# Down projection of a two-layer encoder: plain blocks accumulate on the sum so far in PSUM, and the first mixer's index weights are split by one engine

## The chip, the cores and the metric

The kernel runs on one core of a Trainium2 chip, as one program. The metric is the device time of one execution in microseconds (us), the median of several runs; lower is better.

## What is computed

Two encoder layers over 512 tokens with a model width of 1024. Each layer is half a feed-forward network (FFN), a mixer, a cross-attention to a memory of 256 tokens, and a second FFN half. The change touches the end of all four FFNs and the start of the first mixer:

```python
def swiglu(x, wg, wu, wd):
    return (jax.nn.silu(x @ wg) * (x @ wu)) @ wd      # wd: 2816 x 1024

h = x
for layer in range(2):
    h = h + 0.5 * swiglu(rmsnorm(h, ffn1_norm), wg, wu, wd)
    h = h + mixer(rmsnorm(h, mix_norm), ...)           # layer 0: "even", layer 1: "odd"
    h = h + memory_xattn(rmsnorm(h, mem_norm), rmsnorm(mem, src_norm), ...)
    h = h + 0.5 * swiglu(rmsnorm(h, ffn2_norm), ...)
```

The even mixer starts with `h @ w_in`; the part of `w_in` for the index heads (`iq`, `ik`, `iw`) is the "index weights" below.

## The kernel before

The activations lie transposed: eight tiles `x[d]` of 128 features by 512 tokens, in float32. A float32 product is done as three matmuls on two-part numbers. Each operand is split into a high part (ScalarE rounds it: `wh`, `xh`, `hh`) and a low part (VectorE or GpSimd subtracts: `wl`, `xl`, `hl`), and TensorE sums high by high, high by low and low by high in a PSUM bank. There are eight banks, in two rings of four, `ps_pa` and `ps_pb`. TensorE's instructions keep the order in which the code is written; the other engines' instructions and the DMA issues are put in order when the kernel is built, by a scheduler that weighs readiness and priority. On the chip each engine then runs its own list in that order and waits at its head.

**The FFN.** The 2816 hidden features are 22 blocks, made two at a time: one pair plainly (`plain_pair`, L330), ten pairs with a seven-product scheme on quarters (`product`, L478). The down projection goes over the hidden blocks in three chunks of 8, 8 and 6. The first two chunks use the seven-product scheme and are summed by ScalarE and VectorE into eight SBUF tiles `f.sums[d]` (`gain`, L636 and L638). The third chunk is plain: for each of the eight outputs `d` (the "plain down blocks") `block` loads the 128x768 weights (L163) and splits them (L164, L166), `down_products` runs 18 matmuls into one bank (L718), and `done` finishes with three VectorE instructions:

- L738: `dn = bank + x`, where `x` is the sum of the first two chunks
- L739: `dn = dn * R`, the factor of the norm for each token
- L740: `x = 0.5 * dn + xr`, where `xr` is the residual, loaded back from DRAM

Block 0 is begun inside the last pair; its last two hidden blocks, and those of blocks 1 and 2, come once the pair's hidden values are ready. Then `made` starts the next norm: ScalarE makes `xh` (L212) and the square `sq` (L230), VectorE makes `xl` (L214), and GpSimd adds the squares up in `acc` (L231). SyncE parks each new `x` in DRAM (L186) and loads weights.

**What follows each FFN.** After the first, `mixer0`: five index weight tiles, each against all eight `x` (`index_gemm`, L1143), `x` 0 to 6 first for all three products, then `x` 7. After the second, the next FFN's `plain_pair` (L330): its first group takes the high weights of two tiles with `x` 0 to 3, then 4 to 6, then 7. After the third, `mixer1` (`gemm_nat`, L827), which takes the `x` two by two over many matmuls. After the fourth, the output is stored (L1606).

**Who splits the weights' low part.** `wload` gives it to VectorE, or, where `wshare` is n, every n-th tile to GpSimd (both L166). The table `WS` holds `wshare` for each part of the mixers; `WS[0]` is that of the index weights.

Of the kernel before, what the change touches and what calls it, by code (L numbers as in the profile page):

```python
# [11 lines left out]
F32 = mybir.dt.float32  # L12
# [3 lines left out]
OP = mybir.AluOpType  # L16
# [3 lines left out]
P = 128  # L20
S = 512
# [35 lines left out]
TOP_A = 3  # L57
TOP_B = 2
X_K = 2600
WS = (2, 3, 0, 1, 1, 2, 1, 2, 0, 0, 3, 2, 1, 1, 0, 3)  # L60
FIRST = (0, 1, -1, 2, 3, -2, 4, 5, 6, -3, -4, 7)

PAD_CONST = 24
# [10 lines left out]
HALF = 256  # L74
# [38 lines left out]
class Encoder:  # L113
# [583 lines left out]
    def block(self, c, d, own=False):  # L697

        nc, f = self.nc, self.f
        n = CHUNKS[c] * P  # L700
        src = self.I[f.pre + "wd"][d]
        if not own:
            return self.wload(src, n), self.bank2()
        with self.tc.high_priority():
            w = self.wp.tile([P, 1024], F32, name="wf", tag="wf", bufs=3)
            h, l = [f.tp.tile([P, WIDE], F32R, name=t, tag=t, bufs=1) for t in ("sh", "sl")]
            self.wfill((w, h, l), src, slice(0, n), nc.vector)
        return (h, l), self.bank2()

    def down_products(self, c, block, ops, tail):  # L710

        f = self.f
        (w, bank), nb = block, CHUNKS[c]
        for a, e in ops:
            for j in range(nb - 2, nb) if tail else range(nb - 2):
                b = sum(CHUNKS[:c]) + j
                h = f.H[b // 2][e][:, b % 2 * S:b % 2 * S + S]
                self.nc.tensor.matmul(bank, w[a][:, j * P:(j + 1) * P], h, start=j == a == e == 0,  # L718
                                      stop=j == nb - 1 and (a, e) == ops[-1])

    def reload(self):

# [8 lines left out]
    def down(self, c, first, olds):  # L731

        nc, f = self.nc, self.f

        def done(d, bank):
            x = self.x[d]
            t = f.tp.tile([P, 3 * HALF], F32, name="dn", tag="t")[:, :S]
            nc.vector.tensor_add(t, bank, x)  # L738
            nc.vector.tensor_mul(t, t, f.R)  # L739
            nc.vector.scalar_tensor_tensor(x, t, 0.5, olds[d], op0=OP.mult, op1=OP.add)  # L740
            self.made(d, x)

        early = [first, self.block(c, 1), self.block(c, 2)]
        for ops in (LEAD, REST):
            for b in early[1:]:
                self.down_products(c, b, ops, False)
        for d, b in enumerate(early):
            self.down_products(c, b, LEAD + REST, True)
            done(d, b[1])
        for d in range(len(early), KB):  # L750
            b = self.block(c, d)
            self.down_products(c, b, LEAD + REST, False)
            self.down_products(c, b, LEAD + REST, True)
            done(d, b[1])
# [530 lines left out]
    def xattn(self, pre, mp):  # L1285
# [77 lines left out]
        def gemm():  # L1363
            for h0 in (0, 2):
# [20 lines left out]
                if h0 == 0:  # L1385
                    self.wshare = WS[15]
            yield from self.out_proj(I[pre + "mem_wo"], 4, lambda k: parts[k] if k < len(parts) else None, (2,))
# [89 lines left out]
    def mixer0(self):  # L1477
        pre, I = "l0_", self.I
        with ExitStack() as ctx:
# [13 lines left out]
            def gemm():  # L1493
                iq = []
                self.wshare = WS[0]
                for j in range(4):
# [6 lines left out]
                b = []  # L1503
                yield from self.gemm_nat(b, w[0], xs, WS[1])
                bqk = self.heads(b, v, mp)
                b = []
                yield from self.gemm_nat(b, w[1], xs, WS[2])
                bv = self.values(b, r, P, mp)
                ready.append((bqk, bv))
                b = []  # L1510
                yield from self.gemm_nat(b, w[2], xs, WS[3])
                bqk = self.heads(b, v, mp)
                ready.append((bqk, bv))
                b = []
                yield from self.gemm_nat(b, w[3], xs, WS[4])
                aqk = self.heads(b, v, mp)
# [194 lines left out]
```

## Time and profile before

| what | us |
|---|---|
| median of 3 runs (2058.13 to 2061.13) | 2059.29 |
| the profiled execution | 2058.4 |
| its span, first to last instruction | 2056.6 |
| TensorE busy in the span | 2009.5 |
| VectorE busy | 1660.6 |
| ScalarE busy | 1224.0 |
| GpSimd busy | 395.0 |

TensorE is busy for 98% of the span, so the question of any change is which of its remaining waits it touches. The four plain down stages end at 338, 1060, 1389 and 2052 us of the span; the "first" to "fourth stage" below are these. In lists of instructions, a row is start, duration, engine, line, operation, output <- inputs, shape and count, and in brackets the engine's idle time ahead of it with what ended it.

### The profile page before, as it was taken

How to read it: one execution, taken by the hardware profiler on the slowest of the kernel's cores; microseconds unless marked ns; L12 is line 12 of the kernel's file. 1: busy time of each engine (PE TensorE's matmuls, PEld its weight loads, DVE VectorE, ACT ScalarE, POOL GpSimd, SP SyncE). 2: the span in 40 equal slices, each digit the busy share in tenths (PEclk: the TensorE clock that was granted, in tenths of full speed). 3: DMA queues.
4: the chain of work that ended last, by engine and by line, in shares of the span. 5: the costliest groups of instructions: out<-in, count | busy, mean ns of one | idle time of the engine just before them, and what ended most of it. 6: DMA issues, size and time to landing. Idle time of an engine off the chain costs nothing.

```text
span 2056.6 us, 35616 instructions
## 1 busy us (share of the span) xinstructions
PE 2009.5 (98%) x13982; PEld 1845.5 (90%) x13986; DVE 1660.6 (81%) x2533; ACT 1224.0 (60%) x1874; POOL 395.0 (19%) x352
## 2 busy tenths in 40 slices
PE   8999998999999999999999999999999999999998
PEld 7999997887778889999979999988888888999997
DVE  8979878479876889798799879786568777988976
ACT  6656554475586566565555656444778655666642
POOL 1012003435341211000020010014453122001000
PEclk9999999999999999999999999999999999999999
DMA  8777755322142267777557786835224324767672
GB/s 270 205 198 197 190 167 171 95 77 67 62 134 83 72 185 206 194 195 179 181 168 194 187 211 166 232 113 167 83 83 123 103 82 156 189 183 207 174 219 95
DMA packets 102184, 321.79 MB, mean 156 GB/s; under 512 B 11392, under 2 KB 14592, under 8 KB 102016
## 3 DMA queue, kind: packets, MB, share of 16 engines
q1 hardware_dynamic: 85888, 260.79, 38.3%
q0 software_dynamic: 16128, 58.73, 16.6%
q8 instruction: 110, 1.80, 0.3%
q14 instruction: 58, 0.48, 0.1%
HBM read 304.79 MB, written 14.68 MB: 155 GB/s over the span
## 4 chain that ended last, share of the span: by engine, by line
PE 87%; DVE 9%; ACT 2%; issue 1%; POOL 0%; DMA 0%; SPq 0%; DVEq 0%; ACTq 0%; POOLq 0%
PE ps_pa L478 35%; PE ps_pb L478 15%; PE ps_pa L827 11%; PE ps_pa L778 4%; PE ps_pa L330 3%; PE ps_pb L933 2%; PE ps_pa L718 2%; PE ps_pa L1377 2%; PE ps_pb L718 2%; PE ps_pb L985 1%; PE ps_pa L1224 1%; PE ps_pa L1143 1%; PE ps_pb L958 1%; PE ps_pb L778 1%; DVE xl L214 1%
## 5 line engine op out<-in xcount | busy, mean ns | idle before, releaser
L164 ACT ACTIVATE wh<-wf 128x1024 fp32r<-128x1024 f32 (+2 forms) x147 | 147.4, 1004 | 148.5 <-PE ps_pa L827 30.7
L454 ACT ACTIVATE wh<-s 128x1024 fp32r<-128x1024 f32 x140 | 149.1, 1065 | 124.7 <-PE ps_pa L478 55.9
L455 DVE TENSOR_TENSOR wl<-s,wh 128x1024 fp32r<-128x1024 f32 x140 | 171.3, 1223 | 39.2 <-ACT wh L454 36.7
L454 ACT ACTIVATE wh<-wf 128x1024 fp32r<-128x1024 f32 x124 | 131.9, 1064 | 104.3 <-PE ps_pa L478 52.1
L455 DVE TENSOR_TENSOR wl<-wf,wh 128x1024 fp32r<-128x1024 f32 x124 | 151.2, 1220 | 16.2 <-ACT wh L454 15.9
L166 DVE TENSOR_TENSOR wl<-wf,wh 128x1024 fp32r<-128x1024 f32 (+2 forms) x104 | 118.1, 1140 | 31.5 <-ACT wh L164 29.8
L166 POOL TENSOR_TENSOR wl<-wf,wh 128x1024 fp32r<-128x1024 f32 x43 | 104.4, 2428 | 149.0 <-ACT wh L164 138.2
L454 ACT ACTIVATE sh<-s 128x1024 fp32r<-128x1024 f32 x84 | 89.3, 1064 | 69.2 <-PE ps_pa L478 33.0
L455 DVE TENSOR_TENSOR sl<-s,sh 128x1024 fp32r<-128x1024 f32 x84 | 103.1, 1227 | 33.1 <-ACT sh L454 32.7
L827 PE MATMUL ps_pa<-wh,xh 128*128 128x512 f32 x384 | 123.7, 403 | 0.0
L827 PE MATMUL ps_pa<-wl,xh 128*128 128x512 f32 x384 | 119.8, 393 | 0.4 <-DVE wl L166 0.4
L827 PE MATMUL ps_pa<-wh,xl 128*128 128x512 f32 x384 | 119.9, 394 | 0.0
L478 PE MATMUL ps_pa<-xh,wl 128*128 128x256 f32 x672 | 103.8, 276 | 0.0
L478 PE MATMUL ps_pa<-xh,wh 128*128 128x256 f32 x672 | 103.7, 276 | 0.0
L478 PE MATMUL ps_pa<-xl,wh 128*128 128x256 f32 x672 | 103.6, 276 | 0.0
L231 POOL TENSOR_TENSOR acc<-acc,sq 128x512 f32<-128x512 f32 (+1 forms) x37 | 54.2, 1465 | 255.6 <-ACT sq L230 205.9
L499 POOL DMA_DIRECT2D s<-l_ffn_wq x40 | 35.1, 878 | 310.5 <-DMA s<-l_ffn_wq 172.6
L478 PEld LDWEIGHTS ps_pa<-xh,wh 128*128 128x128 f32 x672 | 89.1, 188 | 0.3
L478 PEld LDWEIGHTS ps_pa<-xh,wl 128*128 128x128 f32 x672 | 88.7, 188 | 0.2
L478 PEld LDWEIGHTS ps_pa<-xl,wh 128*128 128x128 f32 x672 | 88.7, 188 | 0.0
L827 PEld LDWEIGHTS ps_pa<-wl,xh 128*128 128x128 f32 x384 | 72.4, 189 | 17.3 <-DVE wl L166 1.5
L827 PEld LDWEIGHTS ps_pa<-wh,xl 128*128 128x128 f32 x384 | 72.8, 190 | 16.2
(417 smaller groups left out, 6009.0 us busy)
## 6 DMA issues: line engine op xcount, KB each, us to landing
wf<-l_ffn_wq SPq DMA_DIRECT2D x120, 512.0 KB, 4.7
s<-l_ffn_wq SPq DMA_DIRECT2D x80, 512.0 KB, 5.9
s<-l_ffn_wq POOLq DMA_DIRECT2D x80, 512.0 KB, 7.0
wf<-l_ffn_wdq SPq DMA_DIRECT2D x48, 512.0 KB, 3.6
wf<-l_w_in SPq DMA_DIRECT2D x48, 512.0 KB, 3.4
s<-l_ffn_wdq SPq DMA_DIRECT2D x32, 512.0 KB, 4.6
s<-l_ffn_wdq POOLq DMA_DIRECT2D x32, 512.0 KB, 6.9
parked<-x SPq DMA_DIRECT2D x48, 256.0 KB, 2.1
```

Source lines behind the costliest of these rows:

```text
L164: self.leading = nc.scalar.activation(wh[:, sl], w[:, sl], AF.Copy)
L166: eng.tensor_sub(wl[:, sl], w[:, sl], wh.bitcast(F32)[:, sl])
L231: self.summed = (eng or nc.gpsimd).tensor_add(acc[:, :n], acc[:, :n], sq[:, :n])
L330: nc.tensor.matmul(p, w[a][:, k * P:(k + 1) * P], xs[k][c], start=k == order[0] and a == c == 0, stop=k == order[-1] and a == 1)
L454: self.leading = nc.scalar.activation(h, t, AF.Copy)
L455: self.parted = nc.vector.tensor_sub(l, t, h.bitcast(F32))
L478: self.nc.tensor.matmul(bank[:, sl], w[a][:, o:o + P], xs[k][b], start=first and z == a == b == k == 0, stop=z == a == 1 and k == KB // 2 - 1,
L718: self.nc.tensor.matmul(bank, w[a][:, j * P:(j + 1) * P], h, start=j == a == e == 0, stop=j == nb - 1 and (a, e) == ops[-1])
L778: nc.tensor.matmul(banks[dd], a[:, o:o + P], parts(k)[b], start=k == first and a is wh and b == 0, stop=k == last and a is wl)
L827: nc.tensor.matmul(banks[i], xs[k][a][:, i * P:(i + 1) * P], w[b][:, kk * 512:kk * 512 + 512], start=k == a == b == 0, stop=k == KB - 1 an ...
L933: nc.tensor.matmul(bank[:, o:o + n], a, b[:, :n], start=c == 0, stop=c == len(ops) - 1)
L1377: nc.tensor.matmul(p, ws[z][a][:, k * P:(k + 1) * P], xs[k][b], start=k == order[0] and a == b == 0, stop=k == order[-1] and a == 1)
```

## The change

Each plain down block's PSUM bank is filled with `f.sums[d]` by a ScalarE copy ahead of its matmuls (`begun`, L714), and the matmuls add to it. So the addition of L738 goes. VectorE finishes with two instructions: L744 multiplies the bank by 0.5 and R, inside PSUM, and L745 adds the residual from PSUM into `x`. In the first mixer `WS[0]` goes from 2 to 0: VectorE makes the low part of all five index weight tiles.

```diff
-WS = (2, 3, 0, 1, 1, 2, 1, 2, 0, 0, 3, 2, 1, 1, 0, 3)
+WS = (0, 3, 0, 1, 1, 2, 1, 2, 0, 0, 3, 2, 1, 1, 0, 3)
...
         if not own:
-            return self.wload(src, n), self.bank2()
+            return self.wload(src, n), self.begun(d)
...
-        return (h, l), self.bank2()
+        return (h, l), self.begun(d)
+
+    def begun(self, d):
+
+        bank = self.bank2()
+        with self.tc.high_priority():
+            self.nc.scalar.copy(bank, self.f.sums[d])
+        return bank
...
-                self.nc.tensor.matmul(bank, w[a][:, j * P:(j + 1) * P], h, start=j == a == e == 0,
-                                      stop=j == nb - 1 and (a, e) == ops[-1])
+                self.nc.tensor.matmul(bank, w[a][:, j * P:(j + 1) * P], h, start=False,
+                                      stop=j == nb - 1 and (a, e) == ops[-1], skip_group_check=True)
...
         def done(d, bank):
             x = self.x[d]
-            t = f.tp.tile([P, 3 * HALF], F32, name="dn", tag="t")[:, :S]
-            nc.vector.tensor_add(t, bank, x)
-            nc.vector.tensor_mul(t, t, f.R)
-            nc.vector.scalar_tensor_tensor(x, t, 0.5, olds[d], op0=OP.mult, op1=OP.add)
+            nc.vector.scalar_tensor_tensor(bank, bank, 0.5, f.R, op0=OP.mult, op1=OP.mult)
+            nc.vector.tensor_add(x, bank, olds[d])
             self.made(d, x)
```

From the old line 715 on, the change's lines are numbered 5 to 7 higher. TensorE's order stays as it was; the lists of the other engines change near the four stages and in the first mixer's start.

VectorE at the end of the first stage, blocks 6 and 7, before:

```order
L738 TENSOR_TENSOR dn<-ps_pa,x 128x512
L739 TENSOR_TENSOR dn<-dn,R 128x512
L214 SCALAR_TENSOR_TENSOR xl<-x,cols,xh 128x512
L740 SCALAR_TENSOR_TENSOR x<-dn,xr 128x512
L166 TENSOR_TENSOR wl<-wf,wh 128x1024
L738 TENSOR_TENSOR dn<-ps_pb,x 128x512
L214 SCALAR_TENSOR_TENSOR xl<-x,cols,xh 128x512
L739 TENSOR_TENSOR dn<-dn,R 128x512
L740 SCALAR_TENSOR_TENSOR x<-dn,xr 128x512
L214 SCALAR_TENSOR_TENSOR xl<-x,cols,xh 128x512
L231 TENSOR_TENSOR acc<-acc,sq 128x512
```

And there, with the change:

```order
L744 SCALAR_TENSOR_TENSOR ps_pa<-ps_pa,R 128x512
L166 TENSOR_TENSOR wl<-wf,wh 128x1024
L745 TENSOR_TENSOR x<-ps_pa,xr 128x512
L214 SCALAR_TENSOR_TENSOR xl<-x,cols,xh 128x512
L744 SCALAR_TENSOR_TENSOR ps_pb<-ps_pb,R 128x512
L745 TENSOR_TENSOR x<-ps_pb,xr 128x512
L166 TENSOR_TENSOR wl<-wf,wh 128x1024
L214 SCALAR_TENSOR_TENSOR xl<-x,cols,xh 128x512
L231 TENSOR_TENSOR acc<-acc,sq 128x512
L166 TENSOR_TENSOR wl<-wf,wh 128x1024
```

Before, the low part `xl` of block 5 stood between the steps of block 6, and that of block 6 between those of block 7. Now each block's `xl` directly follows its `x`, apart from one index weight tile ahead of the last.

ScalarE in the first stage's last pair, with the change (L714 are the copies; `gs`, `hh` and `gu` belong to the pair's hidden values, `sh` and `wh` are weights):

```order
L557 COPY gu<-ps_pa 128x512
L714 COPY ps_pa<-x 128x512
L164 ACTIVATE sh<-wf 128x768
L561 ACTIVATE gu<-ps_pa 128x512
L164 ACTIVATE wh<-wf 128x768
L714 COPY ps_pb<-x 128x512
L597 ACTIVATE gs<-gs 128x512
L164 ACTIVATE wh<-wf 128x768
L578 ACTIVATE gu<-ps_pa 128x512
L376 ACTIVATE hh<-gs 128x512
L714 COPY ps_pa<-x 128x512
L597 ACTIVATE gs<-gs 128x512
```

The other rows stand there before too, in this order; the three copies are new, and five more stand in the list some 15 rows ahead of these.

ScalarE at the end of the second stage, blocks 5 to 7, before (the 128x1024 tiles are the next FFN's first two weights):

```order
L164 ACTIVATE wh<-wf 128x1024
L212 ACTIVATE xh<-x,cols 128x512
L230 ACTIVATE sq<-x 128x512
L164 ACTIVATE wh<-wf 128x1024
L212 ACTIVATE xh<-x,cols 128x512
L230 ACTIVATE sq<-x 128x512
L212 ACTIVATE xh<-x,cols 128x512
L230 ACTIVATE sq<-x 128x512
```

And there, with the change:

```order
L212 ACTIVATE xh<-x,cols 128x512
L230 ACTIVATE sq<-x 128x512
L164 ACTIVATE wh<-wf 128x1024
L212 ACTIVATE xh<-x,cols 128x512
L230 ACTIVATE sq<-x 128x512
L164 ACTIVATE wh<-wf 128x1024
L212 ACTIVATE xh<-x,cols 128x512
L230 ACTIVATE sq<-x 128x512
```

The first of the two weight tiles stood ahead of block 5's `xh` and now stands behind it; the second stood ahead of block 6's `xh` and now stands behind it.

## The prediction

> **What bounds the kernel now.** I read the page's head and its chain of waits first, then TensorE's waits, then the lists of instructions at the four stages.
>
> ```profile
> PE 2009.5 (98%) x13982; PEld 1845.5 (90%) x13986; DVE 1660.6 (81%) x2533; ACT 1224.0 (60%) x1874; POOL 395.0 (19%) x352
> PE 87%; DVE 9%; ACT 2%; issue 1%; POOL 0%; DMA 0%; SPq 0%; DVEq 0%; ACTq 0%; POOLq 0%
> ```
>
> TensorE is busy in 98% of the span and carries 87% of the chain. Its order and its matmuls stay. So the change can only give back what TensorE waits near the four stages, and the 5 us after its last matmul. Its waits, by what ended them (total, times, longest):
>
> ```profile
> PE ps_pa L330 <- ACT wh L164: 10.5, 4, 7.5
> PE ps_pa L1143 <- ACT xh L212: 5.9, 2, 3.3
> ```
>
> 7.5 of the first row's 10.5 us is one wait at the kernel's start; the second row is the end of the first stage. TensorE at the end of the first, where L1143 is the first index weight tile:
>
> ```profile
> 337.97 1.29 PE L1143 MATMUL ps_pa<-xh,wh 128*128 128x512 f32 x5
> 341.85 0.49 PE L1143 MATMUL ps_pa<-xh,wh 128*128 128x512 f32 x1 [2.58 <-ACT xh L212]
> 345.68 0.80 PE L1143 MATMUL ps_pa<-xh,wh 128*128 128x512 f32 x1 [3.34 <-ACT xh L212]
> 346.27 3.10 PE L1143 MATMUL ps_pa<-xl,wh 128*128 128x512 f32 x7
> 350.83 0.39 PE L1143 MATMUL ps_pa<-xh,wh 128*128 128x512 f32 x1
> ```
>
> Block 7's last matmul is issued just ahead of 337.97 and ends at 338.1. From 337.97 to 350.83 run the 21 matmuls on `x` 0 to 6. Unhindered they stand 0.227 us apart (below, eight take from 1076.24 to 1078.05), so 21 need 4.77 us: **8.1 us are lost**. 5.9 are the two waits in brackets, for `xh` of blocks 5 and 6. Most of the other 2.2 comes of a clock granted at half after them:
>
> ```profile
> 344.00:346.00 2.00, 0.32 (x1) 0.32 (x2) 2.00 (x4) 1.09 (x2) 0.00 (x0) 0.50 0.50 200
> ```
>
> (Columns: stretch, length, TensorE, its weight loads, VectorE, ScalarE, GpSimd, granted clock 0.50, DMA share, GB/s.) In the second stage, 48 matmuls of L330 lead to the group that starts at 1076.24:
>
> ```profile
> 1059.79 1.07 PE L330 MATMUL ps_pa<-xh,wh 128*128 128x512 f32 x4
> 1064.11 1.21 PE L330 MATMUL ps_pa<-xh,wh 128*128 128x512 f32 x4 [2.34 <-ACT wh L164]
> 1068.93 0.50 PE L330 MATMUL ps_pa<-xl,wh 128*128 128x512 f32 x1 [1.52 <-DVE xl L214]
> 1076.24 1.98 PE L330 MATMUL ps_pa<-xh,wh 128*128 128x512 f32 x8
> 1078.05 1.98 PE L330 MATMUL ps_pa<-xl,wh 128*128 128x512 f32 x8
> ```
>
> 48 steps of 0.227 are 10.9 us; it took 16.45: **5.55 us are lost**, 2.34 of it on a weight's high part on ScalarE, 1.52 on block 6's `xl`. The third stage loses one wait:
>
> ```profile
> 1390.45 0.73 PE L827 MATMUL ps_pa<-wl,xh 128*128 128x512 f32 x2 [0.42 <-DVE wl L166]
> ```
>
> Behind all three stands VectorE's queue. VectorE in the first stage, grouped (count, busy, mean ns, idle ahead), then some of its steps and a GpSimd row:
>
> ```profile
> L214 DVE SCALAR_TENSOR_TENSOR xl<-x,cols,xh 128x512 fp32r<-128x512 f32 x8 | 9.9, 1238 | 0.8 <-ACT xh L212 0.8
> L740 DVE SCALAR_TENSOR_TENSOR x<-dn,xr 128x512 f32<-128x512 f32 x8 | 8.6, 1078 | 0.1
> L739 DVE TENSOR_TENSOR dn<-dn,R 128x512 f32<-128x512 f32 x8 | 6.6, 822 | 0.1
> L738 DVE TENSOR_TENSOR dn<-ps_pa,x 128x512 f32<-128x512 f32 x4 | 2.8, 691 | 2.1 <-PE ps_pa L718 2.0
> ```
>
> ```profile
> 315.05 0.69 DVE L738 TENSOR_TENSOR dn<-ps_pa,x 128x512 f32<-128x512 f32 x1 [1.96 <-PE ps_pa L718]
> 338.30 2.74 DVE L740 SCALAR_TENSOR_TENSOR x<-dn,xr 128x512 f32<-128x512 f32 x1
> 344.80 1.21 DVE L166 TENSOR_TENSOR wl<-wf,wh 128x1024 fp32r<-128x1024 f32 x1
> 348.75 0.69 DVE L740 SCALAR_TENSOR_TENSOR x<-dn,xr 128x512 f32<-128x512 f32 x1
> ```
>
> ```profile
> 337.68 2.81 POOL L166 TENSOR_TENSOR wl<-wf,wh 128x1024 fp32r<-128x1024 f32 x1
> ```
>
> VectorE starts block 0 at 315.05 and ends block 7's `x` at 349.44, 34.4 us with 0.8 of idle, while TensorE is through with all eight at 338.1: the last `x` is 11.3 us late. L740 takes 1078 ns on average here. In the fourth stage, where GpSimd has nothing to do, it takes 692:
>
> ```profile
> L740 DVE SCALAR_TENSOR_TENSOR x<-dn,xr 128x512 f32<-128x512 f32 x8 | 5.5, 692 | 0.2
> L739 DVE TENSOR_TENSOR dn<-dn,R 128x512 f32<-128x512 f32 x8 | 5.5, 690 | 0.2
> ```
>
> The long ones stand beside GpSimd rows, as the 2.74 us at 338.30 beside the 2.81 at 337.68. L738, which reads PSUM and one SBUF tile, never is long: 691. So I count L744 and L745, each with one PSUM and one SBUF input, as never stretched.
>
> [...]
>
> **The change, part by part.**
>
> *Three instructions become two.* Starts follow each other at 0.60 us where they are independent and 0.73 where not (the fourth stage's last rows, below), 0.66 on average. Eight fewer: 5.3 us. L744 and L745 have no row: no VectorE instruction of the trace writes PSUM. L738 prices the reading at 0.69, and ScalarE shows what writing does to the same shape:
>
> ```profile
> L544 ACT COPY gu<-ps_pa x40: 554/567/581, 42.5 to 2007.8; 128x512 f32<-128x512 f32 x40
> L525 ACT COPY ps_pa<-ps_pa x36: 578/580/602, 50.7 to 1996.8; 128x512 f32<-128x512 f32 x36
> ```
>
> 580 against 567 ns. So I price both at 0.69, with 0.25 more for the pair as the upper bound, from the spread of L544 to L525 many times over. [...]
>
> *The stretches.* L740's is 8 x (1.078 - 0.692) = 3.1 us and L739's 8 x (0.822 - 0.690) = 1.1. Both are gone unless `xl` and `wl`, which keep two SBUF inputs, meet the GpSimd rows in their stead. Without that, VectorE needs 34.4 - 5.3 - 4.2 = 24.9 us and ends block 7 at 340.0; with all of it (or with L744 and L745 stretched after all), at 344.1. It cannot end before 338.14 + 0.73 + 0.69 = 339.6. I take 341.5, since some of the overlap will move: 3.4 us late in place of 11.3.
>
> *First stage.* Block 6 is then done by about 339, its `xh` is ready when TensorE wants it, near 339.5. `x` 7 is wanted at 338.0 + 4.77 = 342.8. Its `xh` comes 0.7 after `x`, and its `xl` stands behind an index weight's low part (1.21 at 344.80): 343.7. I take 0.6 us lost: **7.5 gained**; bounds 8.1 and, from 344.1, 4.8. Waits of this length leave the clock whole, as those of the second stage did (1.00 behind the wait of 2.34 us):
>
> ```profile
> 1064.00:1066.00 2.00, 1.90 (x8) 1.58 (x9) 2.00 (x2) 0.38 (x2) 1.08 (x1) 1.00 0.61 240
> ```
>
> *Second stage.* Here ScalarE's row decides:
>
> ```profile
> 1061.86 0.72 ACT L212 ACTIVATE xh<-x,cols 128x512 fp32r<-128x512 f32 x1 [3.37 <-DVE x L740]
> 1063.01 1.04 ACT L164 ACTIVATE wh<-wf 128x1024 fp32r<-128x1024 f32 x1
> ```
>
> The weight TensorE waits for stood behind block 5's `xh`. Now it stands behind block 6's `xh` and `sq`. `x` 6 comes some 2.5 us ahead of `x` 7 (two finishing steps, an `xl` and a 128x1024 low part lie between): by the first stage's bounds, from 1.0 before TensorE's end to 3.5 after it. From the start of `xh` to the end of the weight it is 2.2 us (1063.01 + 1.04 - 1061.86), and TensorE wants it after eight matmuls, at 1.8. The wait lies between none and 3.9 us; I take 1.2: **4.3 gained** (1.6 to 5.5).
>
> *Third and fourth.* The 0.4 us wait in the third goes (0 to **0.4**): that low part now stands ahead of block 6's last step. At the end one step goes:
>
> ```profile
> 2051.59 0.69 DVE L738 TENSOR_TENSOR dn<-ps_pb,x 128x512 f32<-128x512 f32 x1 [1.94 <-PE ps_pb L718]
> 2053.04 0.69 DVE L740 SCALAR_TENSOR_TENSOR x<-dn,xr 128x512 f32<-128x512 f32 x1
> ```
>
> The three start 0.73 apart: **0.7** (0.2 to 0.7, if the PSUM pair costs 0.25 to 0.5 more).
>
> *The copies.* Eight of 0.58 us per stage on ScalarE. TensorE needs each before its block, and each stands far ahead. They read sums that are finished with the second chunk, ahead of the last two pairs. Where ScalarE is dense:
>
> ```profile
> 298.77 0.84 ACT L164 ACTIVATE sh<-wf 128x768 fp32r<-128x768 f32 x1 [1.19 <-PE ps_pa L478]
> 307.49 0.63 ACT L597 ACTIVATE gs<-gs 128x512 f32<-128x512 f32 x1 [1.59 <-DVE gs L596]
> 310.22 0.63 ACT L597 ACTIVATE gs<-gs 128x512 f32<-128x512 f32 x1 [0.36 <-DVE gs L596]
> ```
>
> The copy ahead of `sh` fits into the 1.19 us of idle; that of block 7 into the 1.59 us ahead of the first `gs`; that of block 6 has 0.36 us ahead of the second `gs` and pushes it by about 0.2. What follows is the last `hl` on VectorE, and TensorE's use of it:
>
> ```profile
> 312.40 0.69 DVE L377 TENSOR_TENSOR hl<-gs,hh 128x512 fp32r<-128x512 f32 x1 [0.76 <-ACT hh L376]
> 374.11 0.69 DVE L260 TENSOR_REDUCE s<-ps_pb 128x4 f32<-128x512 f32 x1 [14.77 <-PE ps_pb L258]
> ```
>
> ```profile
> 313.95 0.61 PE L718 MATMUL ps_pa<-hl,sh 128*128 128x512 f32 x2
> ```
>
> It ends at 313.09, 0.86 before the use. So the copies cost **nothing**; gone is that cover if they lose over 0.9 us, and then TensorE waits directly, in each of four stages.
>
> *The index weights.* GpSimd's 2.81 us at 337.68 goes, which is part of the stretches above; VectorE takes over three of 1.21 us, in a time when it idles up to 14.77 us (the row at 374.11). Nothing.
>
> Sum: 7.5 + 4.3 + 0.4 + 0.7 = 12.9 us. The profiled execution took 2058.4: 2045.5. The median shown is 0.9 above it: **2046.4**. All the low bounds give 6.6, 2052.7; all the high ones 14.7, 2044.6.
>
> **The rivals.**
>
> *The overlap moves to `xl` and `wl`.* In the first stage every `xl` starts as its `sq` ends and GpSimd wakes, and L214 has the highest mean already, 1238. Then the low bounds hold: gains from 6.6 to 10, about 2051. Against it: a block then costs VectorE two steps, one `xl` and one 128x768 low part, some 2.9 us by starts, while TensorE needs 18 x 0.227 = 4.1; 1.2 us of slack absorbs a stretch. 24%.
>
> *No change.* If work inside PSUM were as slow as the 1.2 us of the 128x1024 rows, the pair would take 2.4 in place of 2.07, VectorE would gain 4.2 and lose 2.7, and 2 to 3 us would be left: 2056.5. The L738 rows speak against it. 8%.
>
> *Slower.* The copies hold ScalarE's queue in the last pair. Two copies stand between its halves, and one takes a bank that VectorE's last addition (L586) must leave first. Beyond the 0.86 us each microsecond is paid four times. To undo the 12.9 and add 4.1 it takes 4.3 + 0.9 = 5.2 us of delay per stage, nine copies' worth, 2063.5 and more. 4%.
>
> **How the numbers follow.** The forecast has 64%, the rivals 24, 8 and 4. A measurement here tells 0.2%, 4.1 us, from no change, so forecast and first rival are faster: 0.88; same 0.08; slower 0.04. The range takes in all the bounds and the runs' own spread of 1 to 2 us: 2043 to 2053.
>
> **What would show it.** The L1143 row after the stage should run without a bracket over 1 us and at clock 1.00, its group for `x` 7 starting about 5.4 us after block 7; the L330 wait for `wh` should be near 1 us; L744 and L745 should have minimum and maximum within 0.05 us of 0.69, also beside GpSimd rows; block 7's `x` should end some 3.4 us after TensorE; the row of `hl` ahead of L725's use should keep 0.5 us. It is wrong if L744 takes over 0.9, if L725 waits for a copy, or if the lost time turns up further on, as waits of L478 or L827 that were not there.

## The result: 15.9 us faster, and the profile after

| | before | after |
|---|---|---|
| median, four runs each | 2059.57 us (2058.13 to 2061.13) | 2043.68 us (2042.16 to 2044.55) |
| ratio, 95% interval | | 0.9922 (0.9905 to 0.9939) |
| profiled execution | 2058.4 | 2043.34 |
| its span | 2056.6 | 2041.6 |

A second series, five runs beside 21 of the kernel before, gave 2043.80 against 2059.64, a ratio of 0.9925 (0.9913 to 0.9938); 14 to 17 us were expected of it. The forecast was 2046.4, the range 2043 to 2053.

The page's head and its chain of waits, after: TensorE is busy 4.4 us less than the 2009.5 before (its mean granted clock is 0.998 in place of 0.996), VectorE 30 us less with 29 instructions fewer, ScalarE 16 us more.

```profile
PE 2005.1 (98%) x13982; PEld 1844.6 (90%) x13986; DVE 1630.7 (80%) x2504; ACT 1240.0 (61%) x1906; POOL 384.6 (19%) x349
PE 89%; DVE 7%; ACT 2%; issue 1%; DMA 1%; POOL 0%; SPq 0%; ACTq 0%; DVEq 0%; POOLq 0%
```

TensorE's waits, after. The row of the index weights on `xh` (5.9 us before) is gone. The row on `wh` has lost 2.4 us: 2.0 in the second stage, and 0.5 in the wait at the kernel's start (7.5 before), which the change does not touch. The row on `xl` was 3.0 us.

```profile
PE ps_pa L330 <- ACT wh L164: 8.1, 4, 7.0
PE ps_pa L330 <- DVE xl L214: 1.2, 4, 0.4
```

TensorE at the end of the first stage, L1148 now being the first index weight tile: 21 matmuls without a bracket, from 339.31 to 344.07, 4.76 us where it was 12.86. The window at this place grants the full clock (1.00, the third number from the right; it was 0.50).

```profile
339.31 1.75 PE L1148 MATMUL ps_pa<-xh,wh 128*128 128x512 f32 x7
...
344.07 0.40 PE L1148 MATMUL ps_pa<-xh,wh 128*128 128x512 f32 x1
```

```profile
344.00:346.00 2.00, 2.00 (x11) 1.61 (x10) 0.77 (x3) 1.21 (x2) 0.14 (x1) 1.00 0.85 266
```

The second stage, first group of L330: from 1051.94 to 1063.50 it takes 11.56 us, where it was 16.45. The wait for the weight's high part is down from 2.34 to 0.37.

```profile
1051.94 1.07 PE L330 MATMUL ps_pa<-xh,wh 128*128 128x512 f32 x4
1054.29 1.20 PE L330 MATMUL ps_pa<-xh,wh 128*128 128x512 f32 x4 [0.37 <-ACT wh L164]
1063.50 1.98 PE L330 MATMUL ps_pa<-xh,wh 128*128 128x512 f32 x8
```

VectorE in the first stage, grouped as before (count, busy, mean ns, idle ahead), then three of its rows. L744 and L745 are never long (675 to 700 ns in all four stages). The long ones now are some of `xl` (972 ns on average, 1308 before) and of the weights' low part (1151, 949 before). And `xl` waits for `xh`, 2.4 us in all, where it did not before: VectorE now has time to spare. `x` 7 ends at 342.25. The first two rows are those of before:

```profile
L214 DVE SCALAR_TENSOR_TENSOR xl<-x,cols,xh 128x512 fp32r<-128x512 f32 x7 | 9.2, 1308 | 0.0
L166 DVE TENSOR_TENSOR wl<-wf,wh 128x768 fp32r<-128x768 f32 x5 | 4.7, 949 | 0.0
```

```profile
L214 DVE SCALAR_TENSOR_TENSOR xl<-x,cols,xh 128x512 fp32r<-128x512 f32 x7 | 6.7, 972 | 2.4 <-ACT xh L212 2.4
L166 DVE TENSOR_TENSOR wl<-wf,wh 128x768 fp32r<-128x768 f32 x5 | 5.8, 1151 | 0.0
L744 DVE SCALAR_TENSOR_TENSOR ps_pa<-ps_pa,R 128x512 f32<-128x512 f32 x4 | 2.8, 693 | 2.0 <-PE ps_pa L725 2.0
L745 DVE TENSOR_TENSOR x<-ps_pb,xr 128x512 f32<-128x512 f32 x4 | 2.7, 683 | 0.0
```

```profile
321.96 1.79 DVE L214 SCALAR_TENSOR_TENSOR xl<-x,cols,xh 128x512 fp32r<-128x512 f32 x1
...
337.24 1.54 DVE L166 TENSOR_TENSOR wl<-wf,wh 128x1024 fp32r<-128x1024 f32 x1
...
341.56 0.69 DVE L745 TENSOR_TENSOR x<-ps_pb,xr 128x512 f32<-128x512 f32 x1
```

The fourth stage ends with two steps:

```profile
2037.24 0.70 DVE L744 SCALAR_TENSOR_TENSOR ps_pb<-ps_pb,R 128x512 f32<-128x512 f32 x1 [2.65 <-PE ps_pb L725]
2037.98 0.69 DVE L745 TENSOR_TENSOR x<-ps_pb,xr 128x512 f32<-128x512 f32 x1
```

Where the time went, between the profiled executions, by TensorE's starts: 8.1 us in the first stage, 4.9 in the second (16.45 - 11.56), 0.7 in the third (its first six matmuls take 1.36 us in place of 2.06, and the wait of L827 on `wl`, 0.42, has no row any more) and 0.7 at the end (from the first finishing step's start to the last one's 0.74 in place of 1.45). That makes 14.4 of the 15.0 us between the two spans. The other 0.6 is the balance of the rest: the change reaches its first index matmul 1.3 us later (339.31 against 337.97), and the parts between the stages give back 1.1, -0.2 and 1.1. Some of the 1.3 is two waits of L478 for `wh` and `wl`, 0.47 and 0.24 us at 174.85 and 176.28, which were not there before; they lie 110 us ahead of the first copy (285.27), and run 9 below, with twice the copies, has neither. Two profiled executions of the changed kernel differ by 1.0 (spans of 2041.6 and 2042.6), so none of the 0.6 is put down to the change.

### The profile page after: what moved, and what is told of

The parts are those of the page before. It is cut to its first block, busy times and chain, and to the rows that moved or that the text cites. A ratio compares the mean times of both kernels' runs of the same rounds, so it can differ in the third digit from the quotient of the medians.

```text
span 2041.6 us, 35601 instructions
## 1 busy us (share of the span) xinstructions
PE 2005.1 (98%) x13982; PEld 1844.6 (90%) x13986; DVE 1630.7 (80%) x2504; ACT 1240.0 (61%) x1906; POOL 384.6 (19%) x349
## 4 chain that ended last, share of the span: by engine, by line
PE 89%; DVE 7%; ACT 2%; issue 1%; DMA 1%; POOL 0%; SPq 0%; ACTq 0%; DVEq 0%; POOLq 0%
PE ps_pa L478 35%; PE ps_pb L478 15%; PE ps_pa L832 11%; PE ps_pa L783 5%; PE ps_pa L330 3%; PE ps_pa L725 3%; PE ps_pb L725 3%; PE ps_pb L938 2%; PE ps_pa L1382 2%; PE ps_pb L990 1%; PE ps_pa L1229 1%; PE ps_pb L963 1%; PE ps_pa L1148 1%; PE ps_pb L783 1%; PE ps_pb L330 1%
## 5 line engine op out<-in xcount | busy, mean ns | idle before, releaser
L166 DVE TENSOR_TENSOR wl<-wf,wh 128x1024 fp32r<-128x1024 f32 (+2 forms) x107 | 125.9, 1180 | 40.5 <-ACT wh L164 38.5
L166 POOL TENSOR_TENSOR wl<-wf,wh 128x1024 fp32r<-128x1024 f32 x40 | 97.2, 2429 | 153.2 <-ACT wh L164 142.4
L478 PE MATMUL ps_pa<-xh,wl 128*128 128x256 f32 x672 | 103.8, 276 | 0.0
L478 PE MATMUL ps_pa<-xh,wh 128*128 128x256 f32 x672 | 103.7, 276 | 0.0
L478 PE MATMUL ps_pa<-xl,wh 128*128 128x256 f32 x672 | 103.6, 276 | 0.0
L478 PEld LDWEIGHTS ps_pa<-xh,wh 128*128 128x128 f32 x672 | 89.1, 188 | 0.3
L478 PEld LDWEIGHTS ps_pa<-xh,wl 128*128 128x128 f32 x672 | 88.7, 188 | 0.1
L478 PEld LDWEIGHTS ps_pa<-xl,wh 128*128 128x128 f32 x672 | 88.7, 188 | 0.0
L832 PEld LDWEIGHTS ps_pa<-wl,xh 128*128 128x128 f32 x384 | 72.3, 188 | 15.9
```

What stands on the lines that cost most here:

```text
L166: eng.tensor_sub(wl[:, sl], w[:, sl], wh.bitcast(F32)[:, sl])
L478: self.nc.tensor.matmul(bank[:, sl], w[a][:, o:o + P], xs[k][b], start=first and z == a == b == k == 0, stop=z == a == 1 and k == KB // 2 - 1,
L832: nc.tensor.matmul(banks[i], xs[k][a][:, i * P:(i + 1) * P], w[b][:, kk * 512:kk * 512 + 512], start=k == a == b == 0, stop=k == KB - 1 an ...
```

## The experiments

Each was run five times or more beside the kernel before, on the same chip. The questions: which of the two savings on VectorE, fewer instructions or no stretches, brings the gain; what the index weights add; whether the stretches that moved to `xl` and `wl` still cost; and what covers the copies.

**1. The down blocks alone.** `WS[0]` stays at 2.

```diff
-WS = (0, 3, 0, 1, ...)
+WS = (2, 3, 0, 1, ...)
```

> The down blocks of the change alone; the first mixer's index weights keep GpSimd. Theory of the prediction (fewer VectorE instructions and no stretched finishing steps both count, the index weights add nothing by themselves): the GpSimd row of 2.81 us near 337.7 stays, but L744 and L745 beside it stay at 0.69, so it stretches at most an xl or a wl; 13.5 to 15.5 us below the kernel before, within 1.5 us of the whole change. Rival (the index weights carry a good part of the first stage's 8.1 us): 8 to 12 us below, with a wait for xh or xl of 1 us or more at the first index weight tile.

Measured: 2044.45 against 2058.95, 14.5 us faster, ratio 0.993 (0.9918 to 0.9943). TensorE in the first stage:

```profile
341.28 1.75 PE L1148 MATMUL ps_pa<-xh,wh 128*128 128x512 f32 x7
...
346.22 0.49 PE L1148 MATMUL ps_pa<-xh,wh 128*128 128x512 f32 x1
347.00 0.50 PE L1148 MATMUL ps_pa<-xl,wh 128*128 128x512 f32 x1 [0.29 <-DVE xl L214]
```

`x` 7 ends 1.2 us later than in the change, measured from the first L1148, and TensorE loses 0.2 us ahead of its group and 0.7 behind it (0.29 in the bracket). The down blocks are the change.

**2. The index weights alone.** The kernel before, with `WS[0] = 0`.

> The index weights of the first mixer by VectorE alone, the down blocks as before. Theory of the prediction: the 2.81 us GpSimd row goes and with it the stretch of L740 at 338.30 (2.74 to 0.69), but three more VectorE rows of 1.21 come into its queue, one of them ahead of the last x: between 1 us slower and 2 us faster than before, all of it in the first stage. Rival (the index weights carry a good part): 3 to 6 us faster, the 3.34 us wait for xh gone and the clock whole.

Measured: 2058.14 against 2058.95, ratio 0.9997 (0.9988 to 1.0006): no difference that can be told. TensorE and VectorE in the first stage:

```profile
342.96 0.50 PE L1143 MATMUL ps_pa<-xh,wh 128*128 128x512 f32 x1 [1.55 <-ACT xh L212]
346.74 0.80 PE L1143 MATMUL ps_pa<-xh,wh 128*128 128x512 f32 x1 [3.28 <-ACT xh L212]
```

```profile
344.18 1.75 DVE L740 SCALAR_TENSOR_TENSOR x<-dn,xr 128x512 f32<-128x512 f32 x1
```

The stretch of 2.74 us is gone: block 5's L740 takes 0.68 at 341.47. But an index weight's low part of 1.21 (340.34) now stands ahead of it. The next GpSimd addition stretched block 5's `xl` before (1.79 at 342.48) and now stretches block 6's L740 (1.75). The wait ahead of block 5's matmul fell by 1.0 us, the one ahead of block 6's stayed.

**3. As few instructions, but through SBUF.** The change with the product written to an SBUF tile, and with `WS[0]` at 2: it is run 1 with this one difference, not the whole change as the text below says. The first step then has PSUM as its input and SBUF as its output, the second reads two SBUF tiles.

```diff
-WS = (0, 3, 0, 1, ...)
+WS = (2, 3, 0, 1, ...)
...
-            nc.vector.scalar_tensor_tensor(bank, bank, 0.5, f.R, op0=OP.mult, op1=OP.mult)
-            nc.vector.tensor_add(x, bank, olds[d])
+            t = f.tp.tile([P, 3 * HALF], F32, name="dn", tag="t")[:, :S]
+            nc.vector.scalar_tensor_tensor(t, bank, 0.5, f.R, op0=OP.mult, op1=OP.mult)
+            nc.vector.tensor_add(x, t, olds[d])
```

> The whole change, but the first finishing step writes its product to an SBUF tile, so that the second reads two SBUF inputs, as the last step did before: as few instructions as the change, and still open to a stretch. Theory of the prediction: the instruction count saves 5.3 us of VectorE a stage, up to 3.1 of stretch come back in the second step; block 7's x ends 343 to 345 in the first stage, and the kernel is 8 to 13 us faster than before. Rival (all of it comes from the stretches): L745 at 1.0 us or more on average and 2 to 5 us faster.

Measured: 2045.04, 13.9 us faster, ratio 0.9932 (0.9919 to 0.9946); a little more than expected. The second step is stretched again in the first stage (869 ns, in run 1 679 to 684), and `x` 7 ends at 343.54, as expected; TensorE waits 0.54 us. Against run 1 that is 0.5 us more lateness of `x` 7 (4.66 for 4.13, table below), and a time that cannot be told from it (13.9 for 14.5).

```profile
L214 DVE SCALAR_TENSOR_TENSOR xl<-x,cols,xh 128x512 fp32r<-128x512 f32 x7 | 8.0, 1142 | 1.6 <-ACT xh L212 1.6
L746 DVE TENSOR_TENSOR x<-dn,xr 128x512 f32<-128x512 f32 x8 | 6.9, 869 | 0.1
```

```profile
344.34 0.49 PE L1149 MATMUL ps_pa<-xh,wh 128*128 128x512 f32 x1 [0.54 <-ACT xh L212]
```

**4. As many instructions, none with two SBUF inputs.** The kernel before, its three steps inside the bank; no copies, `WS[0]` at 2.

```diff
-            nc.vector.tensor_add(t, bank, x)
-            nc.vector.tensor_mul(t, t, f.R)
-            nc.vector.scalar_tensor_tensor(x, t, 0.5, olds[d], op0=OP.mult, op1=OP.add)
+            nc.vector.tensor_add(bank, bank, x)
+            nc.vector.tensor_mul(bank, bank, f.R)
+            nc.vector.scalar_tensor_tensor(x, bank, 0.5, olds[d], op0=OP.mult, op1=OP.add)
```

> The kernel before, but its three finishing steps work in the PSUM bank, so that none has two SBUF inputs: as many instructions as before, none open to a stretch; no copies, index weights by GpSimd as before. Theory of the prediction: 4.2 us of VectorE are saved a stage and block 7's x ends near 345 in the first stage; 5 to 9 us faster than before, and nothing of the 0.7 us at the end. Rival (all of it comes from the stretches): 12 to 15 us faster, both stalls gone. Rival (the count alone): 0 to 2 us.

Measured: 2047.28, 11.7 us faster, ratio 0.9945 (0.9932 to 0.9957): above the 5 to 9 of my theory, just below the rival's 12 to 15. TensorE's wait in the first stage, and the three steps, L737 to L739 here, without a stretch:

```profile
344.50 0.49 PE L1142 MATMUL ps_pa<-xh,wh 128*128 128x512 f32 x1 [1.15 <-ACT xh L212]
```

```profile
L738 DVE TENSOR_TENSOR ps_pb<-ps_pb,R 128x512 f32<-128x512 f32 x4 | 2.8, 690 | 0.0
L739 DVE SCALAR_TENSOR_TENSOR x<-ps_pb,xr 128x512 f32<-128x512 f32 x4 | 2.7, 677 | 0.0
```

By the time alone the first rival stays possible, since the interval is 8.9 to 14.0 us; but it asked for both stalls to be gone, and 1.15 us of waiting is left in the first stage and 0.93 (on `xl`) in the second, and run 3 came to 13.9 with stretches left. So neither rival holds: **each of the two edits by itself brings most of the gain**, and they do not add up. Why is seen below.

**5. No GpSimd additions.** The kernel before, and (run 6) the change, with GpSimd's additions of the squares behind the down blocks left out. Beside the first stage's finishing steps that leaves one GpSimd row in the kernel before, the index weight's (2.88 us at 335.71), and in the change, where all GpSimd rows there are such additions (321.33 to 342.10), none.

```diff
+            if eng is not None or not getattr(self, 'quiet', False):
-            self.summed = (eng or nc.gpsimd).tensor_add(acc[:, :n], acc[:, :n], sq[:, :n])
+                self.summed = (eng or nc.gpsimd).tensor_add(acc[:, :n], acc[:, :n], sq[:, :n])
...
+            self.quiet = True
             self.made(d, x)
+            self.quiet = False
```

> The kernel before without GpSimd's additions of the squares behind the down blocks; the norms after the four stages then lack the squares of all blocks but those that VectorE adds, and the output changes with them. VectorE keeps its three finishing instructions. Theory of the prediction (stretches and count both count): no L740, L739 or L214 over 1.0 us in the four stages but beside the index weight's GpSimd row, block 7's x ends 4 to 6 us after TensorE in the first stage, and the kernel is 9 to 13 us faster than before, without the 0.7 us at the end. Rival (the count is what matters): 5 us faster or less.

Measured, for the kernel before without the additions: 2045.67 against 2059.64, 14.0 us faster, ratio 0.9934 (0.992 to 0.9947), above the 9 to 13 expected. Its VectorE in the first stage (L740 and L741 are the second and third step here):

```profile
L740 DVE TENSOR_TENSOR dn<-dn,R 128x512 f32<-128x512 f32 x8 | 6.8, 847 | 0.1
L741 DVE SCALAR_TENSOR_TENSOR x<-dn,xr 128x512 f32<-128x512 f32 x8 | 5.5, 688 | 0.1
L214 DVE SCALAR_TENSOR_TENSOR xl<-x,cols,xh 128x512 fp32r<-128x512 f32 x7 | 5.2, 743 | 0.0
```

`xl` takes 743 ns in place of 1308 in the same stretch of the kernel before, the last step 688 in place of 1078. The second step's 847 holds the one row beside the index weight's GpSimd row, 1.98 us at 337.16. So the long rows come from GpSimd's additions and that index row, by taking them away.

**6. The change without the GpSimd additions.**

> The changed kernel without GpSimd's additions of the squares behind the down blocks, so that nothing of xl or of the weights' low parts can be stretched there; the norms after the four stages lack most of their squares, and the output changes with them. Theory of the prediction (the stretches that moved to xl and wl are absorbed, TensorE is what bounds): xl at 0.75 throughout, VectorE through with block 7 by 1 to 2 us earlier, and the time within 1 us of the change. Rival (the overlap moved and still costs): 2 to 5 us faster than the change.

Measured: 2043.55 against 2059.14, ratio 0.9924 (0.9911 to 0.9936), the change's own time. `xl` is down from 972 to 749 ns, `x` 7 ends 1.3 us earlier, and the first group of the second stage loses nothing any more (10.88 us for its 48 matmuls), yet that is worth only the 0.66 us that the change still lost there. The first rival, an overlap that moves and goes on costing, had the move right and the cost wrong.

```profile
L214 DVE SCALAR_TENSOR_TENSOR xl<-x,cols,xh 128x512 fp32r<-128x512 f32 x8 | 6.0, 749 | 2.5 <-ACT xh L212 2.4
```

**7. The copies alone.** The kernel before with the copies, the matmuls still starting each block by overwriting.

> The kernel before with the copies into the banks added; the matmuls still begin each block by overwriting, so the copies do nothing but take ScalarE's time. Theory of the prediction: the last hl still ends 0.3 us or more ahead of its use, and the time is within 1 us of the kernel before. Rival (the copies hold ScalarE's queue): 2 us or more slower, with a wait at L718 in each of the four stages.

Measured: 2059.77 against 2059.64, ratio 1.0001 (0.9992 to 1.001). No cost, to within the interval of some 2 us either way, and the last `hl` ends 0.85 us ahead of its use (313.50 against 314.35).

**8. Each copy four times.** The change, with three more copies per bank.

```diff
-            self.nc.scalar.copy(bank, self.f.sums[d])
+            for _ in range(4):
+                self.nc.scalar.copy(bank, self.f.sums[d])
```

> The changed kernel with each copy into a bank made four times over. In the trace of the change the last hl ends 0.86 us ahead of its use. Three more copies of about 0.53 by starts stand ahead of the second gs, 1.6 us. Theory of the prediction (beyond the cover each microsecond is paid in all four stages): hl comes 0.7 to 1.4 us late, a wait on it at L725's matmuls with hl in each stage, and the kernel is 3 to 6 us slower than the change. Rival (the copies have more room than that, or the planner sets them elsewhere): within 1 us of the change.

Measured: 2063.89 against 2059.64, ratio 1.0021 (1.0012 to 1.003): 20.1 us slower than the change, against 3 to 6 expected, so the rival fell as well. TensorE's waits, and its rows ahead of the first stage:

```profile
PE ps_pa L478 <- ACT gu L544: 8.8, 6, 1.9
PE ps_pa L726 <- ACT sh L164: 8.2, 4, 2.7
```

```profile
299.40 0.73 PE L478 MATMUL ps_pa<-t3h,sh 128*128 128x256 f32 x4 [1.87 <-ACT gu L544]
...
305.13 1.35 PE L726 MATMUL ps_pa<-hh,sh 128*128 128x512 f32 x4 [2.73 <-ACT sh L164]
306.28 1.91 PE L726 MATMUL ps_pa<-hl,sh 128*128 128x512 f32 x4
307.99 1.75 PE L726 MATMUL ps_pa<-hh,sl 128*128 128x512 f32 x4
309.58 0.63 PE L478 MATMUL ps_pb<-xh,wh 128*128 128x256 f32 x4
```

```profile
306.00:308.00 2.00, 2.00 (x7) 1.51 (x6) 1.09 (x3) 1.22 (x3) 0.00 (x0) 0.50 0.41 65
```

It isn't `hl` that comes late but, ten microseconds earlier, `gu` (8.8 us of waits in place of 1.3) and `sh` (8.2 in place of 1.9): the extra copies stand among the last pair's high parts, two of them right ahead of `sh`:

```profile
303.21 0.58 ACT L715 COPY ps_pb<-x 128x512 f32<-128x512 f32 x1
303.72 0.58 ACT L715 COPY ps_pa<-x 128x512 f32<-128x512 f32 x1
304.24 0.84 ACT L164 ACTIVATE sh<-wf 128x768 fp32r<-128x768 f32 x1
```

The wait of 2.73 us is then followed by half a clock (0.50 from 306 to 308): 12 matmuls take 4.45 us, in the change 2.86 (301.00 to 303.86). The first stage starts its index matmuls 6.0 us later than the change does (345.35 against 339.31): 1.87 + 2.73 - 0.48 (a wait that the change has too) + 1.59 is 5.71 of it.

**9. Each copy twice.** After run 8 I took the 0.19 us of idle ahead of `sh` to be the true cover, all but used up.

> The changed kernel with each copy into a bank made twice. Four copies each cost 20 us, and TensorE then waited for gu and for sh, not for hl. In the change's trace ScalarE has 0.19 us of idle left ahead of sh, which TensorE awaits already (0.48 us). Theory that the cover lies there and is as good as used up: one more copy pushes sh by 0.3 to 0.9 us in every stage, and the kernel is 1.5 to 6 us slower than the change. Theory of the prediction (the cover is the 0.86 us ahead of hl's use): one more copy fits, within 1 us of the change.

Measured: 2043.16 against 2059.14, ratio 0.9925 (0.9911 to 0.9938): as the change, so that theory fell too. ScalarE around `sh`:

```profile
298.50 0.59 ACT L715 COPY ps_pa<-x 128x512 f32<-128x512 f32 x1
299.24 0.84 ACT L164 ACTIVATE sh<-wf 128x768 fp32r<-128x768 f32 x1 [0.15 <-PE ps_pa L478]
300.00 0.58 ACT L715 COPY ps_pa<-x 128x512 f32<-128x512 f32 x1
```

The second copy simply stands behind `sh` (300.00), where ScalarE has time. So 16 copies a stage fit and 32 do not; where between the two the cover ends wasn't tried.

## Why the prediction was right, and where its numbers were off

The forecast's gain was 12.9 us, and all its upper bounds together 14.7 (2044.6). Measured are 15.9 by the medians and 15.1 between the profiled executions, of which the four places named give 14.4. So the range held only by the 1 to 2 us that it allowed for the spread, and what lies above the 14.4 is luck as far as these runs show. The mechanism held in all four places.

The table puts the runs side by side, each gain against the kernel before in its own series. "x 7 late" is the end of the last finishing step of block 7 less the start of the first index matmul; "lost" is TensorE's time from its first matmul to the group for `x` 7 less 4.77 us in the first stage, and over the 48 matmuls less 10.9 in the second.

| kernel | gain, us | x 7 late | lost, 1st | lost, 2nd |
|---|---|---|---|---|
| before | | 11.47 | 8.09 | 5.55 |
| index weights alone | 0.8 | 10.40 | 6.74 | 5.54 |
| three steps in PSUM | 11.7 | 5.26 | 1.30 | 1.53 |
| before, no GpSimd additions | 14.0 | 5.23 | 1.27 | 0.16 |
| two steps through SBUF | 13.9 | 4.66 | 0.69 | 0.71 |
| down blocks alone | 14.5 | 4.13 | 0.17 | 0.64 |
| the change | 15.8 | 2.94 | 0.00 | 0.66 |
| the change, no GpSimd additions | 15.6 | 1.62 | 0.00 | 0.00 |

- **What bounds, and the mechanism: right.** The first stage follows one line. The matmul on block 7's `xh` can start 0.80 us behind `x` 7 and is due 4.77 us after the first index matmul, so 3.97 us of lateness are free and the rest is lost: 5.26 gives 1.29 (1.30 measured), 5.23 gives 1.26 (1.27), 4.66 gives 0.69 (0.69), 4.13 gives 0.16 (0.17), 2.94 gives none. The 0.80 is read from these four kernels, so their agreement shows that block 7's `xh` is what that matmul starts on in each, no more (in run 5 TensorE had already lost 0.79 us of it to block 6's `xh`). For 11.47 the line gives 7.50 of 8.09, for 10.40 6.43 of 6.74; there the wait for block 6 and the half clock behind it (0.50 from 346 to 348 before, from 347 to 349 in run 2) end later. This is why the two savings do not add up: 7.5 us of lateness had to go, the fewer steps through SBUF took 6.8 of it (run 3), the bank in place of SBUF by itself 6.2 (run 4), both 7.3 (run 1), both with the index weights 8.5, and the last 1.0 of those buys nothing ahead of `x` 7. Nor is run 3 the count alone: where two steps were open to a stretch it leaves one, and the steps' own stretches fall from 4.2 us (3.1 and 1.1 in the prediction) to 1.4 (8 x 0.18).
- **First stage: mis-sized, 7.5 for 8.1.** The term that was off is the wait at the group for `x` 7, 0.6 us with a last `x` 3.4 us after TensorE. `x` 7 came 2.8 after TensorE's end, its `xl` was there at 344.04 for a matmul at 344.31, and nothing was waited for. The upper bound was met. (The 0.8 us of idle that the prediction puts into VectorE's 34.4 lies behind their end, ahead of the `xl` at 350.23; no term uses it.)
- **Second stage: mis-sized, 4.3 for 4.9.** The wait for `wh` was taken at 1.2 us and is 0.37; run 6 shows that what is left, 0.66 with the slower matmuls behind it (1.20 us for four in place of 1.07), goes with the GpSimd additions.
- **Third stage: 0.4 for 0.7. End: as priced, 0.7.** The wait in the third stage went, but the matmuls around it were slower too, which the price and its upper bound left out. The PSUM pair costs nothing extra: L744 took 681 to 700 ns, L745 675 to 693.
- **The stretches: the reading right, the pricing too narrow.** I counted 4.2 us for L740 and L739 and 5.3 for the count as separate terms. With one instruction fewer, the rest met GpSimd elsewhere: in run 3, with the count down and the steps through SBUF, `xl` fell from 1308 to 1142 ns though nothing was done to it, and the index weights' row was 1.7 us long in its stead (1.2 before); run 1 has the same two (1144 ns and 1.7 us). So once the count is down, the bank in place of SBUF takes 0.5 us off `x` 7's lateness, where it took 6.2 by itself. That a finishing step with one SBUF input is not stretched I had read off L738 alone (691 ns). Runs 3 to 6 agree in the first stage: a second step with two took 869 ns on average beside GpSimd's additions (run 3), the steps with one 677 to 698.
- **The copies: cost right, cover wrong.** Nothing, as run 7 shows. But I expected block 6's copy to push the second `gs` by 0.2 us and to leave `hl` 0.5; the copy fits to the hundredth, and `hl` ends at 314.43, still 0.86 ahead of its use at 315.29. And the place I named, with 0.9 us as the point from which TensorE waits and four times each microsecond as the price, was not where it breaks: run 8 breaks at `gu` and `sh`, ahead of it, at 5 us a stage.

```profile
313.74 0.69 DVE L377 TENSOR_TENSOR hl<-gs,hh 128x512 fp32r<-128x512 f32 x1 [0.76 <-ACT hh L376]
```

```profile
315.29 0.62 PE L725 MATMUL ps_pa<-hl,sh 128*128 128x512 f32 x2
```

- **The index weights: right.** 0.8 us alone, within the interval of none, and 1.3 us on top of the down blocks by the medians of two series (15.8 against 14.5), which lies within their intervals too. The first stage's rows show 0.84 (0.17 ahead of `x` 7 and 0.67 behind it).

The change's VectorE no longer bounds the first stage, and 0.66 us of the second is all that the table shows it to lose still; a version that gains on it could not be told from it (0.2% is 4 us).

## What to carry to other kernels

Ask how late the last result may come without anyone waiting, and count savings against that: here 7.5 us of lateness had to go, two edits brought 6.8 and 6.2 of it when each stood by itself, and together they were worth little more than one. Here the steps that read one operand from PSUM and one from SBUF stayed at 0.67 to 0.70 us beside GpSimd; that alone was worth 11.7 us, not much less than the 13.9 of leaving a third of the steps out, and it costs one renamed output. A queue's cover is not the idle time in front of one late consumer: adding work to a priority queue changes the order, so try the added work alone and some multiple of it.

## What the runs showed that I had not expected

- **The VectorE steps that write PSUM were hardly slower here than those that write SBUF.** The same first step takes 694 ns into the bank (the change) and 684 to 687 into SBUF (run 3), on average over 32 instructions each. The addition of a bank and an SBUF tile takes, in the first stage, 687 to 688 into the bank (run 4) and 682 to 691 into SBUF (the kernel before).
- **In these rows a stretch came near to what was left of the other engine's instruction, and it went both ways.** GpSimd and VectorE in run 2, first stage:

```profile
334.20 1.84 POOL L231 TENSOR_TENSOR acc<-acc,sq 128x512 f32<-128x512 f32 x1 [2.58 <-ACT sq L230]
```

```profile
334.14 0.75 DVE L214 SCALAR_TENSOR_TENSOR xl<-x,cols,xh 128x512 fp32r<-128x512 f32 x1
334.80 1.78 DVE L740 SCALAR_TENSOR_TENSOR x<-dn,xr 128x512 f32<-128x512 f32 x1
```

GpSimd starts at 334.20, while an `xl` with two SBUF inputs runs; its addition, 1.29 us in the changed kernel at 332.27, takes 1.84, 0.55 more, where 0.69 of that `xl` was left. The next VectorE step with two SBUF inputs starts at 334.80, when GpSimd's addition had 1.24 left, and takes 1.78, 1.09 more than L740 takes in the fourth stage, beside no GpSimd row (0.69); it ends at 336.58, 0.54 us after GpSimd's end at 336.04. So the rows show both orders, GpSimd starting while VectorE runs (334.20) and VectorE while GpSimd runs (334.80).

- **The length of a wait did not decide whether TensorE slowed to half.** Behind run 8's wait of 2.73 us the clock is 0.50, behind the 2.34 of the kernel before, in its second stage, it is 1.00 (quoted in the prediction). But run 8 waits 1.86 or 1.87 us for `gu` ahead of each of the four stages. Behind the one at 1018.65 four matmuls take 1.05 us in place of 0.62 from 1019.90 on; behind those at 299.40, 1347.16 and 2014.28 the next twenty stay at 0.61 to 0.64 for four. Behind a wait of 2.21 at 2019.49 four of L726 take 2.07 us in place of 1.07 (as at 1024.89).

```profile
1018.65 0.73 PE L478 MATMUL ps_pa<-t3h,sh 128*128 128x256 f32 x4 [1.86 <-ACT gu L544]
...
1020.76 1.05 PE L478 MATMUL ps_pa<-t3h,sh 128*128 128x256 f32 x4
```

So the prediction's "Waits of this length leave the clock whole" is no rule; in the change no wait was left in the first stage to try it. The price of the 2.73 us is 1.6 us beside the wait itself. What decides between waits of one length, no run here shows.
